# A post-norm decoder layer with a mixture of experts on one core: end of the kernel, routing transposes, five experts' blocks and the bias queue changed together

## The chip, the core and the metric

The kernel runs on one NeuronCore of a Trainium2 chip. TensorE (PE) does the matmuls and transposes, VectorE (DVE) and ScalarE (ACT) the elementwise work, GpSimd (POOL) the index work, partition broadcasts and the DMAs that need an index, and SyncE (SP) issues most of the plain DMAs. The metric is device time in microseconds, lower is better.

## The reference, cut to what matters

```python
u = x @ w_in + b_in                      # x is 1024 tokens x 1024, float32
y_attn = sliding_window_sink_attention(q, k, v, sinks) @ w_attn_br
y_conv = conformer_conv(c_in, ...)
merged = gate[..., :D] * y_attn + gate[..., D:] * y_conv
x = layer_norm(ALPHA * x + merged @ w_o, ln1_g, ln1_b)
logits = h @ w_router + b_router         # 32 experts, the 4 best of each token
act = clamped_swiglu(xb @ w_up[e] + b_up[e])      # w_up[e] is 1024 x 2048
y = act @ w_down[e] + b_down[e]                   # w_down[e] is 1024 x 1024
x = layer_norm(ALPHA * x + sum of gate * y, ln2_g, ln2_b)
```

Every expert has 12 MB of float32 weights, and all 32 are read. 1024 tokens times 4 give 4096 token slots.

## The kernel before, in words

**First part.** Projections, attention, convolution, and from about 500 us on eight blocks of 128 tokens through `w_o`, the first layer norm (`ln1`) and the routing. Block `b` runs two halves of 512 columns (`wo_mm(b, 0)`, `wo_mm(b, 1)`, 24 matmuls each); pieces of the routing of block `b - 1` are hung between those matmuls by a count: `T_AT` names the count after which PE transposes the normalised block (`route_T`, four 128x128 transposes for each half of the columns), `RT`, `LOG` and `SEL` those after which come a transpose of ranks (`ranks_T`), the router's logits (`route`) and the choice of the four experts (`select`).

**Experts.** Experts are sorted by their number of tokens, and `CAPS` gives the capacity of each place: 320 slots for the fullest, 64 for the emptiest. A capacity is cut into blocks of 128, 64 and 32 slots (`Expert.__init__`, L114). An expert with a block of 128 has its weights split (`split_w`, L203): ACT copies them to the type fp32r (`hi`), DVE subtracts (`lo`), and a block of 128 takes three matmuls `hi*hi`, `hi*lo`, `lo*hi` in that type. Blocks of 64 and 32 use the raw float32 weights, with two or four groups of columns beside each other on the array, and where an expert has only such blocks (`CAPS` 96 and 64) nothing is split.

An expert is 12 steps of two weight rows-of-128 each (512 KB a row): steps 0 to 3 give the first half of the up columns, 4 to 7 the second, 8 to 11 the down projection. After steps 3 and 7 DVE and ACT do `swiglus`; `act_T` transposes the activations for the down steps; `x_T` transposes an expert's gathered tokens before its first step. I call each group of four steps a phase.

**Order.** `LANES` pairs heavy experts with light ones: between two phases of a heavy expert stand one or two phases of light ones. The first lane has the heavy places 6 to 12 and the light ones 13 to 18 and 31; the second the heavy places 0 to 4 and the light ones 19 to 30; place 5 comes last, alone. With the work units of L58 (12, 8 and 5 for a block of 128, 64 and 32) the loop from L1139 on spreads the light phases. `G` is the list of all steps. `at(g, f)` (L1391) says that `f` is issued behind the matmuls of step `g`; within one step the order is that of `rank_of`. Each engine works through its instructions in that order. `split_ahead` (L1260) issues weight splits up to three steps ahead of PE, and weight loads are issued on SP as soon as the 24 slots of `W` tiles allow (`fits`, L1237).

**Queues.** SP issues the weight loads and the output rows; POOL issues slot tables (`fetch`), token gathers, scatters, and all biases (`load_row`, `load_bias`), and it broadcasts the biases of 128-slot blocks over the partitions (`bias_of`, L232).

**End.** While the last expert (place 5, 256 slots) runs, `fin_load` reads back the 1024 rows of the sum in eight blocks, `fin_stats` and `fin_out` normalise them and SP writes them; the schedule is L1449 to L1454. When the last matmul is done, `fin_slots` adds the last expert's rows to gathered copies of the sum (`fin_gather`), normalises them on DVE, and POOL scatters them over the output.

## Time and profile before

| | |
|---|---|
| three runs | 2125.57, 2125.64 and 2132.51 us, median 2125.64 |
| profiled execution | 2130.01 us, its span 2128.4 us |
| granted TensorE clock, mean over the span | 0.980 |
| PE busy | 2024.0 us (95%) |
| DVE busy | 1373.8 us (65%) |
| ACT busy | 892.8 us (42%) |
| POOL busy | 491.5 us (23%) |
| HBM read and written | 472.95 and 35.46 MB, 239 GB/s over the span |

The span runs from the first to the last instruction; shares are of the span. Matmuls are pipelined and their ends are modelled, so the distance from one start to the next is the real cost of a matmul, not its listed duration. PEclk is the granted clock, 1.00 for 2.4 GHz and 0.5 for 1.2 GHz. An idle time in square brackets stands before the instruction and names what ended it. The table of work over 40 slices shows PE at nine tenths or more in all but a few slices:

```profile
PE   7999999999887999999999989999999999999993
DVE  3768789666775888889899754444435424544475
PEclk9999999999998999999999999999999999999997
```

### The profile page before, as it was taken

What the parts mean: (1) busy time and instruction counts of PE and PEld (TensorE: products, weight loads), DVE (VectorE), ACT (ScalarE), POOL (GpSimd) and SP (SyncE); (2) the same over time, 40 slices, a digit from 0 to 9 for tenths busy, and PEclk for the clock granted to TensorE, in tenths of its full rate; (3) what the DMA queues carried; (4) which work ended last, traced back from release to release, by engine and by line L of the source; (5) the groups of instructions that cost most, each with busy time, mean ns of one, the idle gap of its engine ahead of it and who ended that gap; (6) DMA issues with size and microseconds to landing.
All of it is one profiled execution on the core that took longest, in us unless ns stands there. A gap on an engine that the chain in (4) does not pass through costs nothing. (4 is left out here: it accounts for less than half of the span.)

```text
span 2128.4 us, 31602 instructions
## 1 busy us (share of the span) xinstructions
PE 2024.0 (95%) x10723; PEld 1381.0 (65%) x10723; DVE 1373.8 (65%) x2038; ACT 892.8 (42%) x1368; POOL 491.5 (23%) x665
## 2 busy tenths in 40 slices
PE   7999999999887999999999989999999999999993
PEld 6776788887664677677776755555555555675572
DVE  3768789666775888889899754444435424544475
ACT  3155511332334566566675543222233222332453
POOL 1000000003544131414324313213223223322120
PEclk9999999999998999999999999999999999999997
DMA  6111012132238898989989999979998999989962
GB/s 201 44 40 30 21 45 60 45 113 81 80 109 279 300 322 297 309 292 324 337 290 334 312 363 323 311 275 301 372 386 266 330 297 365 380 290 385 346 243 96
DMA packets 191379, 510.39 MB, mean 240 GB/s; under 512 B 34546, under 2 KB 70692, under 8 KB 191213
## 3 DMA queue, kind: packets, MB, share of 16 engines
q1 hardware_dynamic: 162342, 446.76, 58.6%
q0 software_dynamic: 28320, 59.91, 11.1%
q8 instruction: 85, 1.39, 0.3%
q10 hardware_dynamic: 551, 1.66, 0.2%
q14 instruction: 81, 0.66, 0.1%
HBM read 472.95 MB, written 35.46 MB: 239 GB/s over the span
## 5 line engine op out<-in xcount | busy, mean ns | idle before, releaser
L627 DVE SCALAR_TENSOR_TENSOR c<-a,cw,c 128x1024 f32<-128x1024 f32 x120 | 154.0, 1284 | 3.2
L855 POOL DMA_DIRECT2D bu<-in_b_up_dram x2 | 1.0, 502 | 448.8 <-DVE wol L92 448.8
L146 POOL DMA_DIRECT2D slt<-tab x99 | 57.3, 670 | 22.0 <-issue 6.5
L95 PE MATMUL ga<-xh,whga 128*128 128x512 f32 x128 | 52.1, 407 | 0.0
L97 PE MATMUL ga<-xh,wlga 128*128 128x512 f32 x128 | 50.5, 395 | 0.0
L96 PE MATMUL ga<-xl,whga 128*128 128x512 f32 x128 | 50.5, 394 | 0.0
L97 PE MATMUL gb<-xh,wlgb 128*128 128x512 f32 x128 | 50.4, 394 | 0.0
L95 PE MATMUL gb<-xh,whgb 128*128 128x512 f32 x128 | 50.4, 394 | 0.0
L96 PE MATMUL gb<-xl,whgb 128*128 128x512 f32 x128 | 50.4, 394 | 0.0
L92 DVE TENSOR_TENSOR p1l<-p1w,p1h 128x1024 fp32r<-128x1024 f32 x24 | 28.6, 1231 | 23.8 <-ACT p1h L91 23.2
L92 DVE TENSOR_TENSOR p0l<-p0w,p0h 128x1024 fp32r<-128x1024 f32 x24 | 28.4, 1222 | 22.9 <-ACT p0h L91 22.7
L92 DVE TENSOR_TENSOR p4l<-p4w,p4h 128x1024 fp32r<-128x1024 f32 x24 | 30.3, 1299 | 17.2 <-ACT p4h L91 16.8
L92 DVE TENSOR_TENSOR p2l<-p2w,p2h 128x1024 fp32r<-128x1024 f32 x24 | 29.2, 1242 | 18.6 <-ACT p2h L91 15.5
L92 DVE TENSOR_TENSOR p5l<-p5w,p5h 128x1024 fp32r<-128x1024 f32 x24 | 29.7, 1258 | 16.3 <-ACT p5h L91 8.7
L1048 POOL DMA_INDIRECT tab<-rec,dst x32 | 36.1, 1128 | 15.4 <-POOL rec L1046 8.2
L92 DVE TENSOR_TENSOR p3l<-p3w,p3h 128x1024 fp32r<-128x1024 f32 x24 | 28.8, 1240 | 13.2 <-ACT p3h L91 10.3
L952 PE MATMUL wo<-woh,mh 128*128 128x512 f32 x128 | 36.3, 415 | 0.0
L467 ACT ACTIVATE gt<-ga,pcol 128x512 f32<-128x512 f32 x16 | 11.0, 690 | 59.2 <-PE ga L97 59.1
L952 PE MATMUL wo<-woh,ml 128*128 128x512 f32 x128 | 35.9, 404 | 0.0
L92 DVE TENSOR_TENSOR p12l<-p12w,p12h 128x1024 fp32r<-128x1024 f32 x24 | 28.6, 1231 | 10.2 <-ACT p12h L91 10.0
L670 DVE SCALAR_TENSOR_TENSOR sc<-s,mask 128x512 f32<-128x512 f32 (+1 forms) x32 | 19.5, 652 | 23.9 <-PE s L667 21.8
L952 PE MATMUL wo<-wol,mh 128*128 128x512 f32 x128 | 34.2, 402 | 0.0
(1255 smaller groups left out, 6327.6 us busy)
## 6 DMA issues: line engine op xcount, KB each, us to landing
p6w<-in_w_up_dram SPq DMA_DIRECT2D x16, 512.0 KB
p13w<-in_w_up_dram SPq DMA_DIRECT2D x16, 512.0 KB
p7w<-in_w_up_dram SPq DMA_DIRECT2D x16, 512.0 KB
p14w<-in_w_up_dram SPq DMA_DIRECT2D x16, 512.0 KB
p8w<-in_w_up_dram SPq DMA_DIRECT2D x16, 512.0 KB
p15w<-in_w_up_dram SPq DMA_DIRECT2D x16, 512.0 KB
p9w<-in_w_up_dram SPq DMA_DIRECT2D x16, 512.0 KB
p16w<-in_w_up_dram SPq DMA_DIRECT2D x16, 512.0 KB
```

Of the source, the lines that this page charges most:

```text
L92: nc.vector.tensor_tensor(lo, src, hi.bitcast(F32), op=ALU.subtract)
L95: nc.tensor.matmul(o, ah, bh, start=start, stop=False)
L96: nc.tensor.matmul(o, ah, bl, start=False, stop=False)
L97: nc.tensor.matmul(o, al, bh, start=False, stop=stop)
L146: nc.gpsimd.dma_start(self.m[g * w:(g + 1) * w, i, :], tab[bass.ds(row + c, w), :])
L467: nc.scalar.activation(GT[c][:, sl], t, AF.Sigmoid, bias=bin_c(14 + c))
L627: nc.vector.scalar_tensor_tensor(C[c], A[c][:, w:w + S], cw[:, c, w:w + 1], C[c], op0=ALU.mult, op1=ALU.add)
L670: nc.vector.scalar_tensor_tensor(SC[b][c0 // 2][:, g::2, :W], t[g][:, :, :W], 0.125, mk[:, None, :].to_broadcast([P, 2, W]), op0=ALU.mult, ...
L855: nc.gpsimd.dma_start(bu, b_up[:, i * S:(i + 1) * S])
L952: nc.tensor.matmul(t, ml[:, k, :], W[k][:, sl], start=n == 0, stop=n == 3 * KC - 1)
L1048: i = nc.gpsimd.indirect_dma_start(out=tab[:, :], out_offset=bass.IndirectOffsetOnAxis(ap=DST[b][:, k:k + 1], axis=0), in_=REC[:, b, k, :] ...
```

## The change

Five edits, made together.

1. `T_AT`: the first half's transposes of `route_T` move from behind the 18th to behind the 22nd matmul of `wo_mm(b, 0)`, the second half's from behind its 22nd to behind the first matmul of `wo_mm(b, 1)`; `RT` moves from 2 to 3.
2. `CAPS` and `LANES`: places 19 to 23 have 128 slots where they had 96, so one block of 128 with split weights where they had a block of 64 and one of 32 with raw weights. They move from the second lane to the first, and place 31 from the first to the second. Worked through by the rule of L1134 to L1150, the first lane now runs 7 heavy and 11 light experts, in an order such as `*9.0 18.1 *9.1 18.2 19.0 *9.2 19.1 *10.0 19.2 20.0` (place and phase, a star for heavy), the second 5 heavy and 8 light ones. `act_T` of an expert whose second phase follows directly on its first is issued two steps later.
3. `load_bias` of 64-slot blocks goes to SP's queue.
4. The end: `fin_load` in two DMAs of 64 rows, and earlier for blocks 4 to 7; `fin_blocks` up to two steps earlier; the last multiplication of blocks 6 and 7 on ACT and the addition on POOL (`aside`); block 7's output between the two `fin_slots`; the scatters apart (`fin_scatter`). The two constant rows are loaded in four pieces each.
5. The router's bias has a tile of its own, and the outputs of the last expert use another tile name.

```diff
@@ -43,17 +43,17 @@
 FIRST = 3
 NORD = 7
 MID = 16
-T_AT, RT, LOG, SEL = (18, 22), 2, 6, 9
+T_AT, RT, LOG, SEL = (22, 1), 3, 6, 9
 TQ = 9
 TA, TB, TC, TD, TE = 0, 2, 3, 7, 2
 AHEAD = 6
 BROW, BC, ACTB, XG = 2, 3, 3, 3
 V_AT, S_AT = (2, 3, 4, 5, 7), (0, 3)
 CAPS = [320, 288, 256, 256, 256, 256, 192, 192, 192, 160, 160, 160, 160, 128, 128, 128,
-        128, 128, 128, 96, 96, 96, 96, 96, 64, 64, 64, 64, 64, 64, 64, 64]
-
-LANES = [([6, 7, 8, 9, 10, 11, 12], [13, 14, 15, 16, 17, 18, 31]),
-         ([0, 2, 1, 3, 4], [24, 19, 25, 20, 26, 21, 27, 22, 28, 23, 29, 30])]
+        128, 128, 128, 128, 128, 128, 128, 128, 64, 64, 64, 64, 64, 64, 64, 64]
+
+LANES = [([6, 7, 8, 9, 10, 11, 12], [13, 14, 15, 16, 17, 18, 19, 20, 21, 22, 23]),
+         ([0, 2, 1, 3, 4], [24, 25, 26, 27, 28, 29, 30, 31])]
 LAST = 5
 UNITS = {128: 12, 64: 8, 32: 5}
 TR = 9 * P
@@ -221,10 +221,11 @@
                 if w < P:
                     ng = P // w
                     bg = self.bias[v, i] = self.t(f"bg{w}", f"bg{i}{v}", [P, 8 * w])
-                    src = bud[P if w == 64 else 32][bass.ds(self.ev(nc.gpsimd), 1), v * S:(v + 1) * S].rearrange(
+                    eng = nc.sync if w == 64 else nc.gpsimd
+                    src = bud[P if w == 64 else 32][bass.ds(self.ev(eng if w == 32 else None), 1), v * S:(v + 1) * S].rearrange(
                         "e (g n) -> e g n", g=ng)
                     for g in range(ng):
-                        nc.gpsimd.dma_start(bg[g * w:(g + 1) * w], src[:, g].to_broadcast([w, 8 * w]))
+                        eng.dma_start(bg[g * w:(g + 1) * w], src[:, g].to_broadcast([w, 8 * w]))
 
         def bias_of(self, u):
             if u in self.brow:
@@ -327,7 +328,7 @@
         def scale_out(self, i):
             w = self.blocks[i][0]
             n = D * w // P
-            ys = self.ys[i] = self.t("xl128" if self.tail else f"ys{w}", f"ys{i}", [P, n])
+            ys = self.ys[i] = self.t("al128" if self.tail else f"ys{w}", f"ys{i}", [P, n])
             for h, a in enumerate(self.acc[i]):
                 m = min(n, 512)
                 nc.scalar.activation(ys[:, h * m:(h + 1) * m], a[:, :m], AF.Copy, scale=self.m[:, i, 1:2])
@@ -929,7 +930,7 @@
         nc.sync.dma_start(wr, w_router.rearrange("(k p) e -> p k e", p=P))
         brow = wp.tile([1, NE], F32, name="brow0", tag="brow0", bufs=1)
         nc.sync.dma_start(brow, b_router)
-        brt = slot("A2", "brt", shape=(P, NE))
+        brt = wp.tile([P, NE], F32, name="brt", tag="brt", bufs=1)
         nc.gpsimd.partition_broadcast(brt, brow)
         bdr, bd = slot("O4", "bdr"), slot("O7", "bd", F32R)
         for g in range(3):
@@ -1158,14 +1159,14 @@
             last = b == NB - 1
             if 1 <= b < NB - 2:
                 wo_load(b + 2)
-            wo_mm(b, 0, dict(zip(T_AT, (lambda: route_T(b - 1, (0,)), lambda: route_T(b - 1, (1,))))) if b else {})
+            wo_mm(b, 0, {T_AT[0]: lambda: route_T(b - 1, (0,))} if b else {})
             wo_post(b, 0)
             if b == 1:
                 nc.scalar.activation(bd[:3 * NE], bdr[:3 * NE], AF.Copy)
                 nc.gpsimd.tensor_tensor(bd[NE:2 * NE], bdr[NE:2 * NE], bd[NE:2 * NE].bitcast(F32), op=ALU.subtract)
             if not last:
                 wo_split(b + 1)
-            sel = {RT: lambda: ranks_T(b - 2) if b > 1 else None, LOG: lambda: route(b - 1), SEL: lambda: select(b - 1)} if b else {}
+            sel = {T_AT[1]: lambda: route_T(b - 1, (1,)), RT: lambda: ranks_T(b - 2) if b > 1 else None, LOG: lambda: route(b - 1), SEL: lambda: select(b - 1)} if b else {}
             if not last:
                 wo_mm(b, 1, sel)
                 if b > 1:
@@ -1315,7 +1316,8 @@
         def fin_const():
             for i, ap in enumerate((ln2_g, ln2_b)):
                 t = F["w", i] = mo.tile([P, D], F32, name=f"l2w{i}", tag="xg", bufs=XG)
-                nc.gpsimd.dma_start(t, ap.to_broadcast([P, D]))
+                for c in range(0, D, 256):
+                    nc.gpsimd.dma_start(t[:, c:c + 256], ap[:, c:c + 256].to_broadcast([P, 256]))
             F["s"] = mo.tile([P, 4, NB], F32, name="f_s", tag="f_s", bufs=1)
             while len(kept) < RING + 1:
                 kept.append(wfree.pop())
@@ -1328,9 +1330,10 @@
 
         def fin_load(b, tag=None, pfx="fy"):
             if tag is None:
-                tag = f"W{kept[b % RING]}"
-            FY[b] = mo.tile([P, D], F32, name=f"{pfx}{b}", tag=tag, bufs=1)
-            nc.gpsimd.dma_start(FY[b], yd[b * P:(b + 1) * P, :])
+                tag = f"W{kept[b % RING]}" if b < 6 else "xl128"
+            FY[b] = mo.tile([P, D], F32, name=f"{pfx}{b}", tag=tag, bufs=1 if tag[0] == "W" else 2)
+            for r in (0, 64):
+                nc.gpsimd.dma_start(FY[b][r:r + 64], yd[b * P + r:b * P + r + 64, :])
 
         def fin_stats(b, dve=False):
 
@@ -1350,13 +1353,17 @@
                 nc.scalar.activation(o, y, AF.Square, bias=s[:, 1], accum_out=s[:, 2])
             nc.vector.scalar_tensor_tensor(y, y, s[:, 1], F["w", 0], op0=ALU.add, op1=ALU.mult)
 
-        def fin_out(*bs):
+        def fin_out(*bs, aside=False):
             s = F["s"][:, :, bs[0]:bs[-1] + 1]
             nc.scalar.activation(s[:, 3], s[:, 2], AF.Sqrt, bias=eps_t, scale=1.0 / D)
             nc.vector.reciprocal(s[:, 3], s[:, 3])
             for b in bs:
                 y = FY.pop(b)
-                nc.vector.scalar_tensor_tensor(y, y, F["s"][:, 3, b:b + 1], F["w", 1], op0=ALU.mult, op1=ALU.add)
+                if aside:
+                    nc.scalar.activation(y, y, AF.Copy, scale=F["s"][:, 3, b:b + 1])
+                    nc.gpsimd.tensor_tensor(y, y, F["w", 1], op=ALU.add)
+                else:
+                    nc.vector.scalar_tensor_tensor(y, y, F["s"][:, 3, b:b + 1], F["w", 1], op0=ALU.mult, op1=ALU.add)
                 nc.sync.dma_start(out[b * P:(b + 1) * P, :], y)
 
         def fin_blocks(*bs):
@@ -1364,7 +1371,7 @@
                 if b >= 0:
                     fin_stats(b, b in FDVE)
                 else:
-                    fin_out(~b)
+                    fin_out(~b, aside=~b > 5)
 
         def fin_slots(i):
             y = F["y", i]
@@ -1379,8 +1386,10 @@
             nc.vector.scalar_tensor_tensor(y, y, mv[:, 0:1], F["w", 0], op0=ALU.subtract, op1=ALU.mult)
             nc.vector.reciprocal(s, s)
             nc.vector.scalar_tensor_tensor(y, y, s, F["w", 1], op0=ALU.mult, op1=ALU.add)
+
+        def fin_scatter(i):
             nc.gpsimd.indirect_dma_start(out=out[:, :], out_offset=bass.IndirectOffsetOnAxis(
-                ap=last.gi[:, i:i + 1], axis=0), in_=y, in_offset=None, bounds_check=S - 1, oob_is_err=False)
+                ap=last.gi[:, i:i + 1], axis=0), in_=F["y", i], in_offset=None, bounds_check=S - 1, oob_is_err=False)
 
 
         todo = {}
@@ -1434,7 +1443,7 @@
             q1, q2 = pos[e.pfx, 4], pos[e.pfx, 8]
             for i in range(e.nb):
                 if e.pfx in heavy or e.full:
-                    at(q1 + (1 if e.nb > 1 else 0), e.act_T, 0, i)
+                    at(q1 + (1 if e.nb > 1 else 2 if G[q1 - 1][0] is e else 0), e.act_T, 0, i)
                     at(q2 + (1 if e is last else 0), e.act_T, 1, i)
                 else:
 
@@ -1447,10 +1456,10 @@
         q = pos[last.pfx, 0]
         at(q - 1, fin_const)
         for b in range(NB):
-            at(q + (0 if b < RING else 6 + b // 2), fin_load, b)
+            at(q + (0, 0, 0, 0, 4, 6, 7, 7)[b], fin_load, b)
         at(q + 8, fin_gather)
-        for s, what in ((4, (0,)), (5, (~0, 1)), (6, (~1, 2)), (8, (~2, 3)), (9, (~3, 4, 5)), (10, (~4, ~5, 6, 7)),
-                        (11, (~6, ~7))):
+        for s, what in ((2, (0,)), (3, (~0,)), (4, (1,)), (5, (~1, 2)), (6, (~2, 3)), (7, (~3,)), (9, (4, 5)),
+                        (10, (~4, ~5, 6, 7, ~6))):
             at(q + s, fin_blocks, *what)
         for n, (e, i) in enumerate(blocks):
             if n >= XG:
@@ -1497,8 +1506,11 @@
             load_ahead(g)
             behind(g)
         assert not todo
-        for i in (1, 0):
-            fin_slots(i)
+        fin_slots(1)
+        fin_blocks(~7)
+        fin_scatter(1)
+        fin_slots(0)
+        fin_scatter(0)
         for i in range(2):
             last.scale_out(i)
 
```

## Rows read from the trace of the kernel before

**Rows 1.** Busy time by stage: length, PE, PEld, DVE, ACT, POOL, clock, DMA share, GB/s.
```profile
500.00:660.00 160.00, 128.05 (x665) 93.08 (x665) 98.06 (x255) 52.95 (x90) 70.11 (x124) 0.91 0.32 106
660.00:1285.30 625.30, 612.27 (x3335) 431.01 (x3333) 528.79 (x669) 387.82 (x496) 193.02 (x239) 0.99 0.92 316
1285.30:2019.40 734.10, 727.10 (x4214) 423.58 (x4212) 312.51 (x537) 216.56 (x333) 194.99 (x250) 1.00 0.95 331
2019.40:2094.20 74.80, 69.58 (x305) 56.94 (x304) 58.77 (x76) 49.96 (x80) 14.65 (x19) 0.98 0.63 217
2094.20:2128.40 34.20, 0.47 (x3) 0.05 (x1) 15.10 (x21) 4.54 (x11) 2.01 (x2) 0.57 0.16 65
```
**Rows 2.** Timeline of PE: start, duration, line, operation, tiles, shape.
```profile
1286.34 0.39 PE L268 MATMUL p0u<-p0l,p0xh 128*128 128x512 f32 x1
1286.57 0.39 PE L268 MATMUL p0u<-p0h,p0xl 128*128 128x512 f32 x1
...
1346.41 1.46 PE L314 MATMUL p0aT<-ident,p0act 128*128 128x128 f32 x10
```
**Rows 3.** Matmuls by tile: ns min/median/max, first and last start in us, shapes.
```profile
L277 PE MATMUL p19u<-p19w,p19xr x192: 385/394/643, 1369.7 to 1392.1; 128*32 128x256 f32 x128, 128*64 128x512 f32 x64
...
L277 PE MATMUL p19d<-p19w,p19ar x96: 379/379/643, 1427.5 to 1438.8; 128*32 128x256 f32 x64, 128*64 128x512 f32 x32
...
L277 PE MATMUL p30u<-p30w,p30xr x64: 592/592/643, 1972.9 to 1986.8; 128*64 128x512 f32 x64
```
**Rows 4.** Busy time by pair of experts: 8 and 15, 10/17, 11/18, 12/31.
```profile
851.30:944.40 93.10, 93.10 (x429) 64.71 (x428) 80.81 (x100) 58.58 (x75) 28.54 (x38) 1.00 0.89 300
...
1031.60:1119.20 87.60, 85.68 (x525) 64.53 (x524) 79.34 (x100) 57.69 (x75) 27.96 (x39) 0.98 0.93 321
1119.20:1206.40 87.20, 84.80 (x523) 63.17 (x522) 79.69 (x103) 57.58 (x75) 28.22 (x36) 1.00 0.91 311
1206.40:1285.30 78.90, 72.88 (x467) 41.77 (x466) 45.42 (x67) 32.10 (x46) 25.22 (x34) 0.96 1.02 359
```
**Rows 5.** DVE by line and shape, 1000 to 1210 us: busy, mean ns, idle before.
```profile
L92 DVE TENSOR_TENSOR p17l<-p17w,p17h 128x1024 fp32r<-128x1024 f32 x24 | 29.5, 1285 | 3.5 <-ACT p17h L91 3.3 <-DMA p10w<-in_w_down_dram 0.2
...
L92 DVE TENSOR_TENSOR p17al<-p17aT,p17ah 128x512 fp32r<-128x512 f32 x2 | 1.4, 685 | 0.0
```
**Rows 6.** Busy time of tile p17t's instructions alone: length, DVE, ACT, clock.
```profile
1000.00:1200.00 200.00, 7.18 (x16) 1.78 (x4) 0.99 0.90 308
```
**Rows 7.** Timeline of DVE beside expert 17's first two phases.
```profile
1049.23 5.46 DVE L92 TENSOR_TENSOR p17l<-p17w,p17h 128x1024 fp32r<-128x1024 f32 x4 [0.19 <-ACT p17h L91]
1054.61 4.62 DVE L92 TENSOR_TENSOR p10l<-p10w,p10h 128x1024 fp32r<-128x1024 f32 x4
```
**Rows 8.** Timeline of POOL in the same stretch.
```profile
1049.07 0.80 POOL L232 PARTITION_BROADCAST p17bc<-p17br  x1 [0.93 <-DVE p10act L294]
```
**Rows 9.** Timeline of DVE and PE, second lane, the largest stall.
```profile
1474.41 0.15 DVE L150 CAST gi<-slt 128x1 int32<-128x1 f32 x1 [9.74 <-DMA slt<-tab]
...
1475.87 0.79 PE L268 MATMUL p2u<-p2l,p2xh 128*128 128x512 f32 x1 [3.48 <-DVE p2l L92]
```
**Rows 10.** Timeline of PE and DVE in one routing block.
```profile
585.17 0.63 PE L992 MATMUL hTp<-ident,hb 128*128 128x128 f32 x4 [0.88 <-issue]
...
585.77 0.75 DVE L976 SCALAR_TENSOR_TENSOR hb<-hb,rstd,lbc 128x512 f32<-128x512 f32 x1
```
**Rows 11.** Timeline of POOL and DVE around the last expert and the end.
```profile
2032.45 2.17 POOL L1333 DMA_DIRECT2D fy<-yd  x4 [4.49 <-DMA yd<-p30ys,si]
...
2099.53 0.74 DVE L1373 SCALAR_TENSOR_TENSOR yg<-p5d,slt,yg 128x512 f32<-128x512 f32 x1
...
2111.35 1.00 POOL L1382 DMA_INDIRECT out_dram<-yg,gi  x1 [4.72 <-DVEq L1507]
```
**Rows 12.** POOL by line and shape over the span: busy, mean ns, idle before.
```profile
L1165 POOL TENSOR_TENSOR bd<-bdr,bd 32x1024 fp32r<-32x1024 f32 x1 | 2.4, 2370 | 0.1
...
L227 POOL DMA_DIRECT2D p24bg<-bud x4 | 2.3, 582 | 15.8 <-DVE p0t L288 12.6 <-issue 3.3
```

## The prediction

> **What bounds the kernel now.** I read the views from coarse to fine. Busy time by stage comes first [rows 1]: from 660 to 2094 us PE is busy for 97% of the time, in both lanes of experts. The reader is to see there that DVE differs: 529 of 625 us in the first lane (85%), 313 of 734 us in the second (43%). Next comes what a matmul costs: two starts lie 0.23 us apart while each lasts 0.39 us [rows 2], so I count starts. Then the busy time of one pair of experts after the other [rows 4]: with a heavy expert of 192 slots (8 and 15) PE has no idle time; with one of 160 (10 and 17, 11 and 18) PE is idle for about 2 us, the granted clock falls to 0.98 in one of them, and DVE is busy for 79.34 of 87.6 and 79.69 of 87.2 us, 90.6 and 91.4%. So DVE already sets the pace now and then in the first lane, and that is the lane which the change fills. The last chain is DVE's alone: the last experts' rows start there at 2099.53, five microseconds after PE's last matmul, and the last scatter is issued at 2111.35 [rows 11].
>
> **Five experts of 128 slots, PE's side.** A light expert of 128 slots has 8 up steps and 4 down steps of 12 matmuls, 144 in all: 144 x 0.23 = 33.1 us. Its 16 transposes at 1.46/10 = 0.146 us make 2.3 [rows 2]. Together 35.4. One of 96 took 22.4 us from first to last start of the up steps and 11.3 of the down steps, 34.9 with the length of the last two [rows 3]; its 19 smaller transposes that lie outside cost between nothing and 2.8 at 0.146; I take 1.8, nearer to the full price since they are as many instructions. That is 36.7, so each of the five gains 1.3, 6.5 in all.
>
> What an expert brings to a lane matters more. First lane: a pair of 192 and 128 takes 93.1, so 57.7 for the heavy one; a pair of 160 and 128 has 84.8 us of PE work, so 49.4 [rows 4]. The new first lane asks PE for 3 x 57.7 + 4 x 49.4 + 11 x 35.4 = 760 us. Second lane: it loses 5 x 36.7 = 183.5 and gains expert 31, whose 12 steps cost 12/8 of 14.5 (13.9 between starts, and the last) [rows 3] and some 0.7 of transposes, 22.5.
>
> **DVE's side.** The new blocks need their weights split, and nothing was split for 96. Expert 17 shows the price [rows 5, 6]: 29.5 us of splits, 7.2 of swiglu, 1.4 of activations' splits and, same shape and count, 1.4 for the tokens: 39.5. The heavy experts then cost 80.8 - 39.5 = 41.3 (192) and 79.7 - 39.5 = 40.2 (160) [rows 4]. The new lane asks DVE for 3 x 41.3 + 4 x 40.2 + 11 x 39.5 = 719 us, 94.6% of PE's 760. No pair shows DVE above 91.4%. Its lead over PE is three steps of weights at most, and a swiglu eats most of it; where two light phases now follow each other, DVE owes more than PE gives, and what the heavy down phases give back is capped. So I let DVE set the lane at 91.4%: 719/0.914 = 787 us. Bounds: PE's 760 and 5 us of start (660 to 851.3 is two pairs of 93.1 and 5.1), 765; and the share of the pair 8 and 15, 80.8/93.1 = 86.8%, 828. The 91.4% is the row nearest in kind, a pair in which PE waited for DVE.
>
> First lane: 787 - 625 = +162. Second lane: 734.1 - 183.5 + 22.5 = 573; and less the stall at 1475.9, where DVE waited 9.74 us for a slot table that POOL had issued late and PE then 3.48 us [rows 9]. POOL has far less to issue there: for each 96 it loses 12 bias DMAs and five of six table loads. I take that stall and as much again for the clock, 7 us (bounds 0 and 7, as the same wait may come elsewhere): 566, so -168. The two lanes together: **-6**.
>
> Here a rule speaks against the change. Four splits took 5.46 us while POOL broadcast biases, against 4.62 for the next four [rows 7]; two broadcasts like the one of 0.80 fell into it [rows 8], so each cost DVE about 0.42 of its 0.80. The Trainium skill ("SBUF — State Buffer", Who interferes with whom) states that a DVE instruction with two SBUF inputs and a GpSimd one that reads SBUF exclude each other for the whole instruction. By that rule the twenty added broadcasts would cost DVE 16 us where the row gives 8; the row's price is inside expert 17's 29.5, so the sum would be 8 us higher.
>
> **Routing.** PE stood 0.88 us before the first half's transposes, seen six times of that length, for `hb` [rows 10]. Four matmuls more, 0.92, cover it. But the second half's rows are ready at 585.77 + 0.75 = 586.52, and its new place is only three matmuls (0.69) and four transposes (0.58 at 0.146) behind 585.17, at 586.44, so 0.1 comes back. Seven blocks at 0.88 - 0.1 are 5.5 us; but ACT now rounds the next block before it copies the second half, and the logits that follow may wait for the copy, at worst as long as they gained. I take **-3** (bounds -6, all hidden, and 0, the wait only moved). Nothing waits behind these transposes but the same matmuls.
>
> **Biases on SP.** 32 issues for the eight light experts and 16 for the others go from POOL to SP, 0.58 us each by POOL's row [rows 12], hidden beside PE: **0**. The cover: SP mostly waits for slots. If it is gone, every weight load behind the bias waits: POOL stood 12.6 us for DVE once before such a bias [rows 12]. The new order has a free buffer at nearly all of these places, so I keep 12.6 as the bound.
>
> **End.** After 2094.2 DVE worked 5.3 us on blocks 5 to 7 before the last expert's rows. With blocks 4 to 7 two steps earlier and the last products of 6 and 7 on ACT and POOL, DVE can reach those rows between 2091.4, when block 1 of the expert is complete (12 matmuls before PE's end), and 2099.5 as now; I take 2093.5, since only block 7's statistics then stand before them. From there to the last scatter it is 2111.35 - 2099.53 = 11.8 us, so the scatter comes at 2105.3, 6 us earlier. POOL's addition is priced by the nearest row, 2.4 us [rows 12], ahead of the first scatter, while DVE does the second half, and off the chain. Against it: block 0's statistics come at step 2, which ends near 2019.4 + 3 x 24 x 0.23 = 2036, and its rows were issued at 2032.45 only, once a scatter had landed [rows 11]; ACT may stand there and hold swiglu and PE, for 0 to 4.5 us by the wait for that landing. Fourteen more POOL issues of 0.54 (2.17/4) fall into waits. I take **-5** (bounds -8 and 0). The router bias' tile and the renamed tile: 0, no row waits for either.
>
> **Sum.** -6 - 3 - 5 + 0 = -14 against the profiled execution (2130.0, its span 2128.4), which lies 4.4 above the median of the three; against that median of 2125.6 it is **2111 us**.
>
> **Rivals.**
> - *DVE cannot fill the lane* (slower). Same mechanism, lower share: two light phases in a row empty the lead, each stall also halves the clock for a while. At 88.3% the lane takes 814, at 86.8% 828: 2139 to 2153. It turns to slower below 89.8%, where the lane takes 801. For it: 94.6% of demand. Against it: with heavy down phases DVE catches up.
> - *DVE keeps up.* The lane takes 765: 2089. For it: DVE's gaps in the pairs lie in the heavy down phases, where it had nothing to do. Against it: PE waits at 89 to 91% already.
> - *Nothing at the end and in the routing*: the waits move (second half; block 0's rows). 2119.
> - *Biases late.* SP stands, or the bias lands behind the weights: 12.6 once, 2124. The Trainium skill ("DMA: Bandwidth & Descriptors", Queues, rings and completion order) says an SDMA engine alternates between queue rows, but takes one row's ring in order; so a bias on SP's row sits behind the weights, where POOL's did not. No row here shows it.
> - *Broadcasts block DVE for their full length*, as in the rule above: 2119.
>
> **Chances.** Forecast 0.43 (its own range 2101 to 2121), DVE keeps up 0.18, DVE cannot 0.16, nothing at the ends 0.10, biases late 0.08, full blocking 0.05. The range goes to the fast case and into the slow one: 2087 to 2139. A measurement of this kernel can tell 0.5%, 10.6 us, from no change; below 2115 lie most of the forecast and the fast case, 0.55; above 2136 most of the slow one, 0.12; the rest 0.33.
>
> **What would show it.** First lane between 780 and 795 us, DVE above 90% in it, PE's waits naming the splits of experts 18 to 23; second lane near 566 and no wait above 2 us; no 0.88 before the transposes; last scatter 5 us nearer to PE's last matmul. Wrong if the first lane is below 770 or above 800, or if DVE waits for 64-slot biases.

## The result, and the profile after

The changed kernel takes 2157.37 us (median of four, 2154.54 to 2162.36) where the one before took 2125.61: 1.0151 times as long, 95% interval 1.0136 to 1.0166, some 32 us slower. The forecast was 2111 us, with a range of 2087 to 2139. The profiled execution has 2162.36 us and a span of 2160.8 (before: 2130.01 and 2128.4).

Busy time by stage in the kernel after, with the columns of [rows 1]. The stages begin at the first up matmul of expert 6 (lane 1), of expert 0 (lane 2) and of expert 5 (last expert), and at PE's last matmul.
```profile
650.70:1460.60 809.90, 773.94 (x4033) 573.40 (x4033) 727.16 (x919) 529.84 (x661) 261.29 (x269) 0.98 0.90 312
1460.60:2052.10 591.50, 575.12 (x2768) 366.40 (x2767) 277.94 (x419) 195.90 (x280) 108.69 (x119) 0.98 0.92 315
2052.10:2135.30 83.20, 71.60 (x305) 58.14 (x304) 58.04 (x77) 51.36 (x83) 22.75 (x33) 0.94 0.66 197
2135.30:2160.80 25.50, 0.40 (x2) 0.00 (x0) 12.83 (x19) 5.38 (x9) 6.86 (x4) 0.61 0.20 81
```
The first lane of the kernel before, from the same matmul on ([rows 1] begins it at 660):
```profile
658.90:1285.30 626.40, 613.37 (x3337) 431.87 (x3336) 529.73 (x670) 388.72 (x497) 194.00 (x240) 0.99 0.92 316
```
Lane 1 grew by 183.5 us (forecast 162), lane 2 shrank by 142.6 (forecast 168), and the last expert takes 83.2 instead of 74.9 us. The 46 us between forecast and result are the sum of these differences: 21.5 in lane 1, 25.4 in lane 2, 15 at the end (8.3 and 1.8 lost where 5 were to be won), less 5 that the start gave beyond the 3 forecast and 10.5 of a last stretch that no step touched (below).

PE's longest waits in lane 1 of the kernel after (tile and line, what it waited for, sum, times, longest):
```profile
PE p12aT L315 <- DVE p0xl L92: 4.5, 1, 4.5
PE p11aT L315 <- DVE p22xl L92: 3.9, 1, 3.9
PE p9aT L315 <- DVE p19xl L92: 3.9, 1, 3.9
PE p23u L269 <- ACT p23h L91: 3.0, 1, 3.0
...
PE p6aT L315 <- DVE p14xl L92: 2.2, 1, 2.2
```
Only one of them (`p23u`) names weights, as the forecast had it; the others name `xl`, splits of transposed tokens. Of those waits for `xl`, the kernel before has only the first, with expert 0, in its own first lane:
```profile
PE p12aT L314 <- DVE p0xl L92: 4.4, 1, 4.4
```
How one of the new ones comes about, first on PE, then on DVE, in the kernel after:
```profile
1063.46 1.04 PE L172 MATMUL p19xt<-ident,p19xg 128*128 128x128 f32 x8
1064.33 0.64 PE L315 MATMUL p9aT<-ident,p9act 128*128 128x128 f32 x4
1068.85 0.34 PE L315 MATMUL p9aT<-ident,p9act 128*128 128x128 f32 x1 [3.87 <-DVE p19xl L92]
1068.93 0.68 PE L269 MATMUL p9u<-p9h,p9xh 128*128 128x512 f32 x1
```
```profile
1059.15 0.68 DVE L289 TENSOR_TENSOR p18t<-p18u,p18bc 128x512 f32<-128x512 f32 x1
...
1063.56 4.63 DVE L92 TENSOR_TENSOR p9l<-p9w,p9h 128x1024 fp32r<-128x1024 f32 x4
1068.10 1.28 DVE L92 TENSOR_TENSOR p19xl<-p19xt,p19xh 128x512 fp32r<-128x512 f32 x2
```
In one step PE transposes expert 19's tokens into two of the three "tr" buffers and expert 9's activations into the third; the fifth transpose of `p9aT` needs one back. DVE frees it by `p19xl`, but works in order: first expert 18's swiglu (from 1059.15), then four weight splits. PE stands 3.87 us, and the matmul behind takes 0.68 us where 0.39 is usual (granted clock 0.58 from 1068.9 to 1073.0 us, 1.00 from 1050 to 1063).

The second lane: PE's waits, then DVE's, in the kernel after.
```profile
PE p1u L278 <- DVE p28t L289: 5.5, 1, 5.5
...
PE p0d L278 <- DVE p25t L289: 2.1, 1, 2.1
```
```profile
DVE p25t L289 <- DMA p25bg<-bud: 20.0, 2, 14.2
...
DVE p28t L289 <- DMA p28bg<-bud: 11.0, 1, 11.0
```
DVE waits for 64-slot biases, which the prediction named as a sign that it is wrong. The other such sign, a first lane above 800 us, came too.

The last expert and the end, in the kernel after: ACT and DVE at block 0's statistics, then POOL at the end.
```profile
2075.12 1.06 ACT L1351 ACTIVATE fo<-fy 128x1024 f32<-128x1024 f32 x1 [10.98 <-DMA fy<-yd]
```
```profile
2077.82 1.28 DVE L1354 SCALAR_TENSOR_TENSOR fy<-fy,f_s,l2w 128x1024 f32<-128x1024 f32 x1 [11.91 <-ACT fo L1353]
...
2081.47 0.68 DVE L289 TENSOR_TENSOR p5t<-p5u,p5bc 128x512 f32<-128x512 f32 x1
...
2136.15 0.73 DVE L1380 SCALAR_TENSOR_TENSOR yg<-p5d,slt,yg 128x512 f32<-128x512 f32 x1
```
```profile
2143.66 2.34 POOL L1364 TENSOR_TENSOR fy<-fy,l2w 128x1024 f32<-128x1024 f32 x1 [3.81 <-ACT fy L1363]
2149.98 1.20 POOL L1391 DMA_INDIRECT out_dram<-yg,gi  x1 [3.97 <-SPq L1519]
2154.18 0.98 POOL L1391 DMA_INDIRECT out_dram<-yg,gi  x1 [3.01 <-issue]
```
ACT stands 10.98 us for rows that have not landed, DVE behind it, and PE stands 7.4 us for `p5t`, which stands behind that work in DVE's order. At the end DVE does reach the last rows 0.85 us after PE's last matmul (before: 5.2, [rows 11]), as meant; but POOL's first scatter stands for the addition of block 7 and then 3.97 us for its store, so the last scatter comes 18.0 us after DVE's start on those rows, where 11.8 were forecast, and 18.9 us after PE's last matmul (before: 17.0).

### The profile page after: what moved, and what is told of

It is laid out like the page before. It is cut to its first block, busy times and chain, and to the rows that moved or that the text cites. A ratio compares the mean times of both kernels' runs of the same rounds, so it can differ in the third digit from the quotient of the medians.

```text
span 2160.8 us, 30377 instructions
## 1 busy us (share of the span) xinstructions
PE 2037.9 (94%) x9973; PEld 1467.5 (68%) x9973; DVE 1534.0 (71%) x2166; ACT 1015.3 (47%) x1480; POOL 486.1 (22%) x577
## 5 line engine op out<-in xcount | busy, mean ns | idle before, releaser
L146 POOL DMA_DIRECT2D slt<-tab x74 | 46.7, 797 | 13.8 <-issue 4.2
L1049 POOL DMA_INDIRECT tab<-rec,dst x32 | 36.1, 1127 | 15.2 <-POOL rec L1047 8.2
L671 DVE SCALAR_TENSOR_TENSOR sc<-s,mask 128x512 f32<-128x512 f32 (+1 forms) x32 | 19.5, 653 | 24.0 <-PE s L668 21.8
L92 DVE TENSOR_TENSOR p20l<-p20w,p20h 128x1024 fp32r<-128x1024 f32 x24 | 28.5, 1238 | 8.4 <-ACT p20h L91 8.4
L92 DVE TENSOR_TENSOR p14l<-p14w,p14h 128x1024 fp32r<-128x1024 f32 x24 | 29.3, 1277 | 6.3 <-ACT p6ys L334 4.9
```

The lines of the kernel that those rows point to most:

```text
L92: nc.vector.tensor_tensor(lo, src, hi.bitcast(F32), op=ALU.subtract)
L146: nc.gpsimd.dma_start(self.m[g * w:(g + 1) * w, i, :], tab[bass.ds(row + c, w), :])
L671: nc.vector.scalar_tensor_tensor(SC[b][c0 // 2][:, g::2, :W], t[g][:, :, :W], 0.125, mk[:, None, :].to_broadcast([P, 2, W]), op0=ALU.mult, ...
L1049: i = nc.gpsimd.indirect_dma_start(out=tab[:, :], out_offset=bass.IndirectOffsetOnAxis(ap=DST[b][:, k:k + 1], axis=0), in_=REC[:, b, k, :] ...
```

## Experiments

All kernels by stage, from such windows of each one's profile: start of lane 1, lengths of the lanes and of the last expert, from PE's last matmul to the last scatter, from there to the end of the span, and the median time (us). All but the median come from one execution of each kernel. The first part of e8, e9 and e11 is the same, and lane 1 starts at 653.0, 649.8 and 654.4 us in them, so a difference of a few microseconds in one start shows nothing.

| kernel | start | lane 1 | lane 2 | last | to scatter | close | median |
|---|---|---|---|---|---|---|---|
| before | 658.9 | 626.4 | 734.1 | 74.9 | 17.0 | 17.1 | 2125.6 |
| after | 650.7 | 809.9 | 591.5 | 83.2 | 18.9 | 6.6 | 2157.4 |
| e1 lanes only | 654.5 | 806.6 | 567.9 | 76.4 | 15.3 | 9.7 | 2136.2 |
| e2 rest only | 649.8 | 628.0 | 742.5 | 84.7 | 18.9 | 11.9 | 2137.6 |
| e3 bias by POOL | 649.4 | 809.4 | 567.9 | 84.1 | 18.5 | 10.9 | 2139.2 |
| e4 later transposes | 646.8 | 793.5 | 588.6 | 83.7 | 18.4 | 6.2 | 2144.2 |
| e5 old end | 656.7 | 810.1 | 585.3 | 76.5 | 15.4 | 16.6 | 2161.7 |
| e6 DVE relief | 649.6 | 786.4 | 591.8 | 83.8 | 19.6 | 6.9 | 2139.1 |
| e7 bias early | 650.0 | 808.7 | 574.5 | 84.0 | 18.9 | 6.1 | 2143.2 |
| e8 lanes, e4, POOL | 653.0 | 793.0 | 567.4 | 76.5 | 15.2 | 9.5 | 2123.3 |
| e9 overflow later | 649.8 | 791.1 | 569.4 | 76.5 | 15.1 | 9.5 | 2115.0 |
| e10 POOL's code | 653.0 | 626.1 | 730.9 | 74.9 | 16.9 | 17.3 | 2120.9 |
| e11 e9 and relief | 654.4 | 772.5 | 569.4 | 74.8 | 16.9 | 9.5 | 2098.3 |
| e12 combined | 648.8 | 783.2 | 568.9 | 77.5 | 14.3 | 10.0 | 2105.3 |
| e13 routing only | 651.7 | 625.7 | 731.6 | 76.4 | 15.4 | 17.1 | 2120.6 |
| e14 bias by SP only | 658.9 | 627.8 | 746.3 | 77.5 | 14.2 | 10.0 | 2134.8 |
| e15 lead of four | 646.9 | 950.5 | 573.0 | 73.7 | 17.5 | 9.5 | 2274.1 |
| e16 lead of two | 647.7 | 825.3 | 569.6 | 78.7 | 15.2 | 9.6 | 2146.6 |

**e1 and e2, the change cut in two.** To the kernel before, in e1:
```diff
-LANES = [([6, 7, 8, 9, 10, 11, 12], [13, 14, 15, 16, 17, 18, 31]),
...
+LANES = [([6, 7, 8, 9, 10, 11, 12], [13, 14, 15, 16, 17, 18, 19, 20, 21, 22, 23]),
...
-                    at(q1 + (1 if e.nb > 1 else 0), e.act_T, 0, i)
+                    at(q1 + (1 if e.nb > 1 else 2 if G[q1 - 1][0] is e else 0), e.act_T, 0, i)
```
with `CAPS` of the change; in e2 the same lines backwards in the kernel after.

> The kernel before with only the five 128-slot blocks, the new lanes and the later act_T of two light phases in a row. Theory 1 (the lanes themselves lose, because in the first lane transposes queue behind DVE): first lane about 802 us again, second lane 734 - 161 = 573 (no bias on the sync queue), so 2125.6 + 177 - 161 = about 2142. Rival 2 (the lanes gain the 6 us that the sum gave them, and the loss comes from the biases on the sync queue and from the end): about 2119, first lane near 787.

> The kernel after with the old capacities and lanes; routing, biases by the sync queue and the end are new. Theory 1: routing saves 2 us, late biases cost 5 to 15, the end about 0, so 2128 to 2139. Rival 2 (these edits make up the whole loss of 32 us): above 2150. Rival 3 (they are harmless, as forecast): 2117.

Measured: 1.0052 (1.0034 to 1.0069) and 1.0061 (1.0039 to 1.0082). Both halves lose, 11 and 12 us. With biases by POOL the second lane is 567.9 us, where 566 was forecast; the first is, within 3.3 us, as long as in the kernel after. Together they lose 32, not 23: late biases cost more in the new lanes (e14, below).

**e3, biases by POOL.**
```diff
-                    eng = nc.sync if w == 64 else nc.gpsimd
...
-                        eng.dma_start(bg[g * w:(g + 1) * w], src[:, g].to_broadcast([w, 8 * w]))
+                        nc.gpsimd.dma_start(bg[g * w:(g + 1) * w], src[:, g].to_broadcast([w, 8 * w]))
```


> The kernel after with the 64-slot blocks' biases issued by POOL again. Theory 1 (a bias on the sync queue lands behind the weights that were issued before it): DVE no longer waits 9 to 14 us for p25bg, p26bg, p28bg, p29bg, PE's waits of 5.5, 2.1 and 1.7 us go with the slower clock behind them: 2157 - 14 = 2143. Rival (POOL then issues them as late as in the kernel before, and PE waits for them there): 2157.

Measured: 2139.2, ratio 1.0057 (1.0037 to 1.0077); lane 2 falls by 23.6 us:
```profile
1458.80:2026.70 567.90, 565.68 (x2768) 361.65 (x2766) 278.75 (x419) 196.35 (x280) 125.44 (x153) 1.00 0.94 327
```
That is more than PE's waits. Against the row of the kernel after, 9.4 of the 23.6 us are PE's busy time, 575.1 instead of 565.7 us for the same 2768 matmuls, at a granted clock of 0.98 instead of 1.00; the other 14.2 are its waits. The biases also hold up the weights behind them. The sync queue around expert 25 in the kernel after, and in e3:
```profile
1543.99 1.75 SPq L228 DMA_DIRECT2D p25bg<-bud  x2
1547.00 8.40 SPq L192 DMA_DIRECT2D p0w<-in_w_down_dram  x6
```
```profile
1517.24 21.70 SPq L192 DMA_DIRECT2D p25w<-in_w_up_dram  x16
1539.91 10.78 SPq L192 DMA_DIRECT2D p0w<-in_w_down_dram  x8
```
When and by whom the same bias was issued in e3, and how long it took to land:
```profile
L227 POOL DMA_DIRECT2D p25bg<-bud x4: 516/549/597, 1520.4 to 1531.5; - x4
...
DMA to landing us min/median/max: 6.8/8.3/9.4
```
Counted from the lane's start (1458.8 in e3, 1460.6 after) POOL issues the first at 61.6 us, the sync queue at 83.4, behind the up weights of expert 25, whose issue takes over 20 us as slots come free; and `p0w`'s last load is issued 2.9 us later.

**e7, biases early in the sync queue's order; e14, the same edit in the old lanes.**
```diff
-                at(q - 4, e.load_bias, v)
+                at(q - (4 if any(w == 32 for w, c in e.blocks) or e.pfx in heavy else 8), e.load_bias, v)
```


> The kernel after with the biases of the light 64-slot experts still issued by the sync queue, but four steps earlier in its order. Theory 1 (the sync queue stands for weight slots, so a bias in its order is issued some 25 us later than POOL issued it): second lane falls from 591 to about 570, 2157 - 20 = 2137. Rival (the transfer itself is slow behind the weights on that queue's ring, or its writes disturb DVE): less than half of that, 2147 or more.

> The kernel before with the 64-slot blocks' biases issued by the sync queue and nothing else. Theory (a bias stands in the sync queue's order behind weight loads that wait for slots): second lane from 734 to about 742, DVE waits of 10 us and more for p25bg and p28bg, 2125 + 9 = 2134. Rival (it costs only where the second lane is as dense as in the new order): 2126.

Measured in e7: 1.0091 (1.0074 to 1.0108), lane 2 574.5, so 17.0 of the 23.6 us were the place in the order. DVE no longer waits for any of these biases, so the 6.6 that remain are not waits for biases; it stands twice for weights, 4.5 us each for `p2w` and `p4w`, as it does not in e3. In e14, alone in the kernel before, biases on the sync queue cost 1.0044 (1.0028 to 1.0060), lane 2 12.2 us longer, with waits of 24.4 and 21.2 us of DVE for `p25bg` and `p28bg`. The rival, that it costs something only in the dense new lanes, falls; they double its price.

**e4, light experts' tokens transposed one step later.**
```diff
-                    tpos[e.pfx, i] = heavy_before(p0[n]) + 2 - e.nb + i
+                    tpos[e.pfx, i] = heavy_before(p0[n]) + (3 if e.full else 2) - e.nb + i
```


> The kernel after with the tokens' transposes of light 128-slot experts one step of four later, away from the step in which the heavy expert's activations are transposed. Theory 1a (the loss of the first lane is the collision of two transposes in three PSUM buffers while DVE works off a swiglu and four splits): PE's six waits of 1.3 to 3.9 us for token splits go, and the slower clock behind them: first lane about 780, 2157 - 20 = 2137. Rival 1b (DVE is short over the whole lane, so any wait removed comes back at the next split): first lane 795 or more, 2150 to 2157.

Measured: 2144.2, 1.0087 (1.0070 to 1.0104), lane 1 793.5, 16.4 less. PE at the place shown above:
```profile
1055.50 0.74 PE L315 MATMUL p9aT<-ident,p9act 128*128 128x128 f32 x5
1058.83 1.03 PE L172 MATMUL p19xt<-ident,p19xg 128*128 128x128 f32 x8
```
All five transposes run at once. The collision was real, and a place was its cause, for DVE does the same work (724.5 us, 727.2 in the kernel after); but 793.5 is nearer to the rival's 795 than to the theory's 780, so something is left.

**e6 and e11, less work for DVE** in the kernel after and in e9.
```diff
+                if self.pfx in ("p19", "p20", "p21", "p22", "p23"):
...
+                    lo = hi
+                    nc.scalar.activation(hi, self.raw[s][h], AF.Copy)
+                else:
...
```


> The kernel after, in which experts 19 to 23 leave out the subtraction that makes the low part of their weights and multiply with the high part in its place: DVE has 5 x 29.5 = 147 us less to do, PE's work is the same. Theory 1 (the first lane loses through DVE, by the collision or over the whole lane): it falls from 807 to between 765 and 780 us, 2157 - 33 = 2124. Rival (something else holds the lane, weights that land late or ACT's high parts): it stays above 800, 2150 or more.

> The kernel of e9 in which experts 19 to 23 leave out the subtraction for their weights' low part and multiply with the high part in its place, 147 us of DVE less. It tells whether DVE's density still costs once the collisions are gone. Theory 1 (DVE's share caps the lane near 91%): first lane falls from about 783 to 765 or less, 2113 - 18 = 2095. Rival (only the collisions cost): within 5 us of e9.

Measured: 1.0073 (1.0056 to 1.0090) and 0.9876 (0.9861 to 0.9891). In e6 lane 1 is 786.4, short of the theory's 780, since `p9aT` (3.7 us) and `p6aT` (2.7) still wait for token splits at a DVE share of 75%. In e11, with the collision gone, 772.5, 18.6 less than e9 (18 were expected, though from a base 8 us lower), and PE busy for 759.0 us (I had asked 760 of it). So both hold: the collision costs 12 (e6 to e11, less the overflow's 1.9) to 16 us (e4) whatever DVE has to do, and DVE's density some 19 more.

**e5, the old end** in the kernel after: all of the change from `fin_const` on undone.
```diff
-        for s, what in ((2, (0,)), (3, (~0,)), (4, (1,)), (5, (~1, 2)), (6, (~2, 3)), (7, (~3,)), (9, (4, 5)),
...
+        for s, what in ((4, (0,)), (5, (~0, 1)), (6, (~1, 2)), (8, (~2, 3)), (9, (~3, 4, 5)), (10, (~4, ~5, 6, 7)),
```

> The kernel after with the end of the kernel before. Theory 1 (statistics of block 0 at step 2 make ACT, and behind it swiglu and PE, stand for rows that land late): PE's wait of 7.4 us before p5u goes, the last expert takes 75 us instead of 83, and the last scatter comes 15 to 17 us after PE's last matmul instead of 19: 2157 - 10 = 2147. Rival (the new end is worth 5 us as forecast): 2162.

Measured: 2161.7, ratio 1.0177 (1.0156 to 1.0198): not faster, and the time that the rival gave. By stages the theory holds where the edit acts (last expert 6.7 us shorter, last scatter 3.5 sooner), and lane 2 is 6.2 shorter too, which I can't explain; but 6.0 are lost at the start and 10.0 in the close. My sum had no term for either. Some 4 of the start are POOL's (e10), the rest lies within the spread of starts named above.

**e10, POOL's code.** The kernel before, with this behind the last broadcast:
```diff
+            nc.gpsimd.tensor_tensor(F["s"][:, 0, 0:1], F["s"][:, 0, 0:1], F["s"][:, 0, 0:1], op=ALU.add)
```


> The kernel before with one small addition by POOL behind its last partition broadcast, and nothing else. In the profiles with the new end POOL's first affine select starts at 1.9 us, in those with the old end at 11 to 12, as if POOL still held from the execution before the code that it used last. Theory 1: PE's first transpose comes at 5 us instead of 11.9, routing starts 3.4 us earlier, 2123.4 - 4 = 2119.5. Rival (the early start comes with another part of the new end): 2123.4, first transpose at 11.9.

Measured: 0.9980 (0.9971 to 0.9989). POOL's first steps in the kernel before, then in e10:
```profile
11.53 0.28 POOL masks.py:199 TENSOR_SCALAR_AFFINE_SELECT ident<-ident 128x128 f32<-128x128 f32 x1 [9.94 <-issue]
...
21.25 0.28 POOL L552 PARTITION_BROADCAST sinks<-srow  x1 [8.61 <-issue]
```
```profile
1.89 0.28 POOL masks.py:199 TENSOR_SCALAR_AFFINE_SELECT ident<-ident 128x128 f32<-128x128 f32 x1 [0.30 <-POOL mask L547]
```
One instruction near the end of the program takes a stall off its start, as if the execution before left POOL ready: the identity is ready 9.6 us sooner, PE's first transpose starts at 5.1 instead of 11.9. The new end has this from its additions on POOL: in all ten profiles of kernels with such an addition near the end the first affine select starts at 1.9 us, in the other eight at 10.8 to 12.3.

**e13, routing alone** in the kernel before, with the two lines that use it and the tile of `brt`.
```diff
-T_AT, RT, LOG, SEL = (18, 22), 2, 6, 9
+T_AT, RT, LOG, SEL = (22, 1), 3, 6, 9
```

> The kernel before with the routing of the kernel after alone (second half of the transposes among the next matmuls, the router bias in a tile of its own). Theory (the forecast's step): the wait of 0.88 us before the first half goes in seven blocks, some of it comes back before the second half: 2125 - 4 = 2121. Rival (the wait only moves to the second half or to the logits): 2125.

Measured: 0.9977 (0.9968 to 0.9986), 4.9 us, by the interval 3.0 to 6.8. Transposes of one block in the kernel after:
```profile
578.63 0.63 PE L993 MATMUL hTp<-ident,hb 128*128 128x128 f32 x4
580.03 0.66 PE L993 MATMUL hTp<-ident,hb 128*128 128x128 f32 x4
```
Neither half has an idle time before it; of the 0.88 [rows 10] nothing came back before the second half. Six waits of the logits for ACT, 1.3 us in all in the kernel after, are new.

**e8, the parts that hold, put together.** Edits of e3, e4 and e5 in the kernel after.

> The lanes and the routing of the kernel after, with the light experts' tokens transposed one step later, the biases issued by POOL and the end of the kernel before. By the losses measured one by one (2136 for the lanes alone, 13 back by the later transposes, some 4 for routing): 2119, first lane about 792, second 568, last expert 75. Rival (gains don't add up, since the waits come back at the next splits): 2130, no better than the kernel before.

Measured: 2123.3, 0.9996 (0.9987 to 1.0006). The stages came as expected, the time 4 us above it; its profiled execution, span 2114.6, was the shortest of ten. So these parts together are no faster than the kernel before.

**e9, overflow later.**
```diff
-            if g == 200:
+            if g == 232:
```


> The kernel of e8 (lanes, later transposes, routing, biases by POOL, old end) with the overflow bookkeeping, 7 us of small DVE instructions that stand at step 200, moved to step 232. In the new lanes step 200 has come to lie in the first lane, in the old ones it lay in the second. Theory 1 (where DVE has no time left, 7 us more of it are 7 us and more of PE): PE's waits for p12l, p23h and p0xl, 8 us in all, shrink, first lane from 793 to about 783, 2123 - 10 = 2113. Rival (those waits belong to other work): no change, 2123.

The first of these instructions on DVE in the kernel before, and then the first and last in the kernel after:
```profile
1431.07 0.19 DVE L1279 TENSOR_TENSOR over<-scnt_ps,capr 128x32 f32<-128x32 f32 x1 [12.70 <-PE p19d L277]
```
```profile
1395.98 0.18 DVE L1280 TENSOR_TENSOR over<-scnt_ps,capr 128x32 f32<-128x32 f32 x1
...
1402.80 0.17 DVE L1306 CAST xci<-xcol 128x2 int32<-128x2 f32 x1
```
Step 200 was in the second lane, where DVE had stood idle for 12.70 us, and is in the first since that lane has 216 steps: 7.0 us of DVE with no idle time before them. Measured: 0.9959 (0.9944 to 0.9974). Between profiles lane 1 fell by 1.9 us only: the waits for `p12l` and `p23h` went, that for `p0xl` grew from 4.3 to 5.7. So the time came out as theory 1 had it (8.3 us lower, 10 expected) and its lane did not (1.9 of 10); where the rest of the 8.3 lies, these two profiles don't show.

**e12, combined.** On e9, the first transposes of three-block experts one step later, and of the new end only this, for blocks 6 and 7:
```diff
+                    nc.scalar.activation(y, y, AF.Copy, scale=F["s"][:, 3, b:b + 1])
+                    nc.gpsimd.tensor_tensor(y, y, F["w", 1], op=ALU.add)
```


> The kernel of e9 with two more moves: the first transposes of the experts with three blocks one step later (PE's wait of 4.3 us for p0xl), and the last products of blocks 6 and 7 on ACT and POOL, the rest of the end as before. Expected: 2113 - 4 (transposes) - 2 (two products of 1.2 us off DVE's last chain) - 4 (POOL's code at the start) = 2103. Rival (the gains don't add up): 2113 or more.

Measured: 2105.3 (2102.97 to 2110.38), 0.9914 (0.9899 to 0.9929): 20 us faster than before and 52 faster than after. Lane 1 takes 783.2 (7.9 less; the wait of 5.7 for `p0xl` is gone):
```profile
648.80:1432.00 783.20, 764.87 (x4030) 568.80 (x4030) 720.91 (x884) 528.94 (x661) 244.05 (x283) 0.99 0.93 322
```
It starts only 1 us sooner, where POOL's code should have given 4, but e9's start is the earliest of the three named above; POOL's first affine select does start at 1.9. The last scatter comes 14.3 us after PE.

**e15 and e16, DVE's lead**, on e12.
```diff
-AHEAD = 6
+AHEAD = 8
```
(4 in e16.)

> The kernel of e12 with weights split four steps ahead instead of three. Theory (DVE's short lead caps its share in the first lane): first lane from 783 to about 775, 2105 - 8 = 2097. Rival (split weights hold their slots longer, weights are loaded later): the same or slower, 2105 to 2115, with waits of DVE or ACT for weights.

> The kernel of e12 with weights split two steps ahead instead of three. Theory (a short lead caps DVE's share): first lane from 783 to 795 or more, 2117 or more. Rival (the lead does not matter, or freeing slots earlier helps): 2105 or less.

Measured: 1.0694 (1.0671 to 1.0718) and 1.0100 (1.0084 to 1.0115). PE's longest wait in e15:
```profile
PE p14d L268 <- ACT p14ah L91: 9.7, 1, 9.7
```
What ACT does ahead of it, and the largest sum of ACT's waits for one expert's weights in lane 1 of e15:
```profile
810.09 1.06 ACT L91 ACTIVATE p14h<-p14w 128x1024 fp32r<-128x1024 f32 x1 [5.38 <-DMA p14w<-in_w_down_dram]
...
826.21 0.59 ACT L91 ACTIVATE p14ah<-p14aT 128x512 fp32r<-128x512 f32 x1
```
```profile
ACT p8h L91 <- DMA p8w<-in_w_up_dram: 13.7, 10, 2.7
```
My theory fell on one side: two steps cost 42 us of lane 1, but four cost 167. ACT rounds activations that PE needs at once only behind weights that PE needs later, and it stands for those weights: its waits for weight loads in lane 1 come to some 230 us in e15 and to 2.6 in e12. That is the sign which the rival named, at far more than its price of 10 us; its reason, that split weights hold their slots longer, I did not test by itself. The lead is a place in in-order queues, not a stock.

## Why the prediction was wrong

**Five experts of 128 slots, DVE's side** is the first step that failed: "I let DVE set the lane at 91.4%: 719/0.914 = 787 us." DVE's work was nearly right (719 us forecast, 727.2 from expert 6's first matmul, 720.3 in e9 without the overflow work), PE's too (760 forecast, 759.0 busy in e11). The share was not a property of DVE: I took it from one pair [rows 4] in which a light phase follows each heavy one, and in the new order token transposes meet a heavy expert's activations behind a swiglu and four splits. The share came out at 727.2/809.9 = 89.8%, the very share at which the rival "DVE cannot fill the lane" put no gain and no loss, with a lane of 801 us; DVE's 8 us more make that 810, and the rest of the loss comes from the other terms. One step's move gives back 16.4, the overflow work (a step number that the diff doesn't touch) and expert 0's transposes together 9.8: e12 has 783.2, below the forecast, with a share of 92.0%. Part of that is luck: the wait for expert 0's transposes, 4.4 us, stood in the kernel before as well, and I had not priced its removal.

**Biases on SP, 0**, failed by its reason: "The cover: SP mostly waits for slots." A queue that waits in order is no cover; what stands behind the wait is as late as the wait is long. Here a bias was issued 21.8 us after the time at which POOL issued it. The price was 23.6 in the new lanes, nearly twice my bound of 12.6, and I gave that rival 0.08. The Trainium skill ("DMA: Bandwidth & Descriptors", Queues, rings and completion order) states that one row's ring is taken in order. In e2 biases on the sync queue landed 9.2 to 12.9 us after their issue (four tiles, in the old lanes), in e3 on POOL's in 4.8 to 8.6 (medians of five tiles), which fits it without showing it; e7 shows that the order in which SP issues costs more, 17.0 of 23.6.

**End, −5**, failed: "ACT may stand there and hold swiglu and PE, for 0 to 4.5 us" was the right place with too small a bound (the landing was 10.98 away, PE's wait 7.4), taken from a wait of POOL's for another transfer [rows 11]. That the scatter must wait for the last block's store, 3.97 us, I did not see: I priced the store's chain as ending before the scatter. The time of e5 does not show this, since the old end's close is 10.0 longer there; the stages do.

**Second lane, −168**: right without the biases (734.1 − 567.9 = 166.2). **Routing, −3**: 4.9 measured; the 0.1 that I took off was not there, and of the delay behind ACT no more shows than the six waits of 1.3 us. **Rivals**: three of them came true together (of the third, its half on the end), and I had priced them as exclusive; their sum, 2111 + 15 + 13 + 5 (15 is the first one's price at the share that came out), is 2144, outside the range. The rival of broadcasts that block DVE for their full length asked 8 us more of DVE; the 720.3 of e9, 1.3 above my sum, speak against it. "Busy for 97% of the time" in the first paragraph is 98% by [rows 1]; nothing hangs on it.

Not settled: the close, 6.1 to 17.3 us from the last scatter's issue to the end of the span. It repeats in some kernels that are alike (17.1, 17.3, 17.1 in before, e10, e13; 9.5 in e8, e9, e11, e15), but e14, which is the kernel before with biases on SP, has 10.0; with one profile each I can't tell whether it hangs on the program. Nothing in the profiles shows what runs there. With the close of the kernel before, the change would have lost some 10 us more.

## What to carry to other kernels

When work is moved between stages, ask of each in-order queue what will now stand in front of the one item that PE needs next; a busy share says how likely a collision is, not where it lies, and a queue that waits is a bad place for a small transfer that is needed soon. Look for steps that are placed by number: they move with the order though the diff doesn't touch them. Price rivals as losses that can add up.

## What the runs showed of the hardware

In the kernel before, POOL stood 7 to 10 us without a visible instruction before its first affine select (9.94), partition broadcast (8.61) and iota (7.08), as if code were loaded at a change of kind; no row shows the loading itself:
```profile
33.80 0.47 POOL L562 IOTA it<- 96x384 f32 x1 [7.08 <-issue]
```
The Trainium skill ("GPSIMD Engine Reference", Instruction dispatch) states about 6 us for the first call of freshly loaded code, with nothing in the profile; the rows agree that nothing is shown, and are longer. What e10 adds: one addition by POOL near the end of the program takes the first of these stalls off the start of an execution, worth 4.3 us here (by the interval 2.3 to 6.2). That what POOL ran last in the execution before decides this is the simplest reading; no row shows it directly.
